# The last conv block's taps as fp32r products on TensorE, and the taps of the last two blocks dealt anew

## The chip, the cores and the metric

The kernel runs on one core of a Trainium2 chip. A core has five engines with a queue each, and every queue is worked through in its own order: TensorE (PE in the profile, with PEld for the loading of its weights), VectorE (DVE), ScalarE (ACT), GpSimd (POOL) and SyncE (SP). They wait for each other on semaphores. The metric is the device time of one execution in microseconds (us), the median of several runs.

## What is computed

A trunk of two layers on 256 tokens of width 2048, all in float32. Layer 0 mixes tokens with a Conformer convolution module, layer 1 with latent attention; each is followed by a squared-ReLU MLP. The change lies in the convolution module of layer 0:

```python
def conv_module(h, w_pw1, b_pw1, w_dw, b_dw, ln_g, ln_b, w_pw2, b_pw2):
    u = h @ w_pw1 + b_pw1
    a, gate = jnp.split(u, 2, axis=-1)
    u = a * jax.nn.sigmoid(gate)
    u = depthwise_causal_conv(u, w_dw, width=31) + b_dw
    u = jax.nn.silu(layer_norm(u, ln_g, ln_b))
    return u @ w_pw2 + b_pw2
```

The depthwise convolution gives, for each of the 2048 channels, the sum of 31 taps: each is that channel's row of u, shifted by 0 to 30 tokens, times a weight of its own. The LayerNorm behind it is over all 2048 channels of a token, so nothing behind it can start before the last channel is done.

## The kernel before

Large products run on TensorE in fp32r. A float32 operand x is split into an upper part hi (ScalarE, a copy into fp32r, `upper_half`) and the rest lo = x - hi (`lower_half`), and a product is three of fp32r parts: hi by hi, lo by hi, hi by lo.

The convolution module goes through 16 blocks of 128 channels. In pass c of the loop (c = 1 to 16) TensorE computes both halves of the pointwise product for block c (`conv_mm`, 96 products of 256 columns; the second half starts with row 8), while the other engines work on the block before:

- `glu(c - 1)`: ScalarE takes the sigmoid of the gate (`sg`) and copies the other half (`vb`), GpSimd multiplies them into `ub`, a row of 30 zeros and 256 tokens. For blocks 0, 14 and 15 VectorE does the last step itself (L844).
- The 31 taps of the block are dealt out. ScalarE starts two sums in PSUM with taps 0 and 1 (`start_sum`, L880) and computes a few side products into SBUF (`tp`, `SIDE`: one per block, 2 for block 13, 4 for block 14), which GpSimd adds up (`side_sum`). VectorE adds the others one by one into the two sums (`add_tap`, L910); the last step of the second sum goes into `half` in SBUF, and GpSimd adds the side products to that (`side_join`). At the end VectorE adds the first sum and `half` into `ca` (L918). `SECOND_END` says how many taps are left for the first sum when the second one ends; these are done in the next pass, alternating with the next block's.
- ScalarE and GpSimd split the weights for the coming products (`conv_half`, 8 rows of two loads to a half: `hi` on ScalarE, `lo` on GpSimd).
- Now and then the finished blocks are transposed (`to_tokens`) for the LayerNorm's mean and variance (`ln_stats`: on ScalarE for blocks up to 13, with `bn_stats` on VectorE for 14 and 15).

Block 15 has no product of a later block beside it. 15 of its taps are therefore done on TensorE: ScalarE prepares 15 diagonal matrices `dg` (the identity, scaled by the tap's weight, L862; 8 in pass 13, 7 in pass 14), and TensorE multiplies each, in plain float32, with `ub` shifted (L873), summing in PSUM. ScalarE starts the sum with tap 15, VectorE adds taps 16 to 23 to it in turn with the rest of block 14, and ScalarE and GpSimd make and add the last 7. VectorE puts the three together (`half` at L1163, `ca` at L1166); then come the transposes and statistics of blocks 14 and 15, the mean and the reciprocal deviation (`rsqrt`), which TensorE spreads over the partitions (`spread`, L1213), normalisation and swish, and the product with `w_pw2` (L1287), whose first weights were split at the end of pass 15.

The instructions of the module stand in the order in which the code is written (`tc.manual_schedule()`): each engine's queue has the order of the calls, whichever engine they are for. An engine whose next instruction waits does nothing else. Since `dve_taps(c - 1)` puts all the steps of a pass on VectorE's queue at once, VectorE and ScalarE can be at different passes at the same time.

## Time and profile before

| | us |
|---|---|
| median of 3 runs (1933.84 to 1935.36) | 1934.36 |
| the profiled execution's own time | 1934.31 |
| its span | 1932.5 |
| pass 13 begins: ScalarE's `sg` for block 12 | 163.10 |
| VectorE's `ub` for block 15 | 198.87 |
| first product with `w_pw2` (L1287) | 210.61 |

Times are from the start of the span. The profiled execution took 1.8 us more than its span, and 0.05 us less than the median. A row of the timeline reads: start, length, engine, line and operation, output and inputs with their shapes, how many of the same stand in a row, and in brackets how long the engine stood idle before and what ended that. Lengths of neighbouring instructions overlap a little: an engine begins the next one before the last one's result is out. A row of the chain of waits reads: start, length, engine and output. A row of the table by stretches has, for each engine, the busy time with the number of instructions, then TensorE's granted clock (1.00 is full speed), the share of the DMA engines and GB/s.

### The profile page before, as it was taken

Reading aid. Unit: us, or ns where it says so; the run is one execution under the profiler, and the core shown is the slowest. Engines: PE = TensorE matmul, PEld = TensorE weight load, DVE = VectorE, ACT = ScalarE, POOL = GpSimd, SP = SyncE. Lnnn points to the kernel's source line nnn. Section 1 sums busy time; section 2 is a strip of 40 time slices with the busy share of each in tenths; the row PEclk is TensorE's granted clock in tenths of the full one; section 3 lists DMA queues with packets and bytes.
Section 4 is the critical chain, followed back from the end, with each engine's and each line's share of the span. In section 5 each row is a group of like instructions: output and inputs, shape, how many; then the busy total and the mean of one; then the engine's idle time right before and its main releaser. Section 6 shows DMA issues by size and latency. Waiting matters only on the chain.

```text
span 1932.5 us, 28477 instructions
## 1 busy us (share of the span) xinstructions
PE 1921.0 (99%) x10725; PEld 1681.5 (87%) x10725; DVE 1592.2 (82%) x2457; ACT 1095.6 (57%) x1636; POOL 249.0 (13%) x208
## 2 busy tenths in 40 slices
PE   9999999999999999999999999999999999999998
PEld 8999888888888888888898998888888888888887
DVE  7999988877999776799976766877789987678998
ACT  5667755554555545555576655555555554455554
POOL 6999200000010100000001420000000010000000
PEclk9999999999999999999999999999999999999999
DMA  7766456665585866655656545465646776665774
GB/s 230 214 183 189 153 189 206 193 194 177 175 251 194 263 195 187 194 174 196 217 176 175 142 134 192 155 216 186 188 162 225 222 248 212 191 196 175 231 219 150
DMA packets 230427, 375.50 MB, mean 194 GB/s; under 512 B 16392, under 2 KB 107792, under 8 KB 230032
## 3 DMA queue, kind: packets, MB, share of 16 engines
q1 hardware_dynamic: 224640, 363.28, 58.7%
q0 software_dynamic: 4320, 7.87, 2.2%
q10 hardware_dynamic: 1328, 2.52, 0.4%
q8 instruction: 84, 1.38, 0.3%
q14 instruction: 55, 0.45, 0.1%
HBM read 363.68 MB, written 2.10 MB: 189 GB/s over the span
## 4 chain that ended last, share of the span: by engine, by line
PE 97%; DVE 2%; DMA 0%; ACT 0%; issue 0%; ACTq 0%; DVEq 0%
PE acc L655 24%; PE acc L205 15%; PE acc L203 15%; PE acc L204 15%; PE acc L656 13%; PE acc L823 8%; PE acc L1287 2%; DVE sum L910 1%; DMA xs<-in_x 0%; PE acc L1535 0%; PE acc L1566 0%; PE acc L1565 0%; PE acc L1536 0%; PE acc L1564 0%; PE acc L1537 0%; PE tr L267 0%
## 5 line engine op out<-in xcount | busy, mean ns | idle before, releaser
L174 DVE TENSOR_TENSOR lo<-raw,hi 128x1024 fp32r<-128x1024 f32 (+2 forms) x509 | 602.2, 1197 | 232.3 <-ACT hi L170 226.6
L170 ACT ACTIVATE hi<-raw 128x1024 fp32r<-128x1024 f32 (+2 forms) x574 | 583.9, 1036 | 361.1 <-PE acc L655 203.7
L655 PE MATMUL acc<-xt,hi 128*128 128x512 f32 x2048 | 710.6, 390 | 0.0
L656 PE MATMUL acc<-xt,lo 128*128 128x256 f32 x2048 | 577.5, 282 | 0.0
L655 PEld LDWEIGHTS acc<-xt,hi 128*128 128x128 f32 x2048 | 384.3, 188 | 80.7
L656 PEld LDWEIGHTS acc<-xt,lo 128*128 128x128 f32 x2048 | 387.1, 189 | 0.2
L497 ACT ACTIVATE hi<-raw 128x1024 fp32r<-128x1024 f32 x248 | 228.7, 948 | 228.3 <-DVE raw L505 134.0
L498 DVE TENSOR_TENSOR lo<-raw,hi 128x1024 fp32r<-128x1024 f32 x248 | 263.9, 1087 | 27.6 <-ACT hi L497 22.5
L203 PE MATMUL acc<-hi,sh 128*128 128x512 f32 x514 | 200.1, 389 | 0.0
L205 PE MATMUL acc<-lo,sh 128*128 128x512 f32 x514 | 200.1, 389 | 0.0
L203 PE MATMUL acc<-hi,gh 128*128 128x512 f32 (+1 forms) x516 | 200.0, 388 | 0.0
L205 PE MATMUL acc<-lo,gh 128*128 128x512 f32 (+1 forms) x516 | 199.9, 387 | 0.0
L204 PE MATMUL acc<-hi,gl 128*128 128x512 f32 (+1 forms) x516 | 199.9, 387 | 0.0
L823 PE MATMUL acc<-xt,hi 128*128 128x256 f32 x1024 | 180.2, 281 | 0.3 <-ACT b L1106 0.2
L204 PE MATMUL acc<-hi,sl 128*128 128x512 f32 x450 | 175.1, 389 | 0.0
L578 POOL DMA_DIRECT2D xs<-v x30 | 26.5, 994 | 1136.4 <-DVE lo L174 703.2
L910 DVE SCALAR_TENSOR_TENSOR sum<-ub,w_dw,sum 128x256 f32<-128x256 f32 x409 | 164.3, 481 | 3.6 <-ACT sum L880 3.0
L174 POOL TENSOR_TENSOR lo<-raw,hi 128x1024 fp32r<-128x1024 f32 x65 | 155.0, 2410 | 17.3 <-ACT hi L170 17.3
L823 PEld LDWEIGHTS acc<-xt,hi 128*128 128x128 f32 x1024 | 154.8, 188 | 1.1 <-ACT xt L1090 0.6
L823 PE MATMUL acc<-xt,lo 128*128 128x256 f32 x512 | 139.2, 279 | 0.0
L205 PEld LDWEIGHTS acc<-lo,sh 128*128 128x128 f32 x514 | 96.5, 188 | 20.4 <-DVE lo L498 0.3
L204 PEld LDWEIGHTS acc<-hi,gl 128*128 128x128 f32 x516 | 96.9, 188 | 19.9
(314 smaller groups left out, 2531.3 us busy)
## 6 DMA issues: line engine op xcount, KB each, us to landing
raw<-in_mlp_w SPq DMA_DIRECT2D x255, 1024.0 KB, 5.5
raw<-in_conv_w_pw SPq DMA_DIRECT2D x62, 512.0 KB, 5.1
raw<-in_conv_w_pw SPq DMA_DIRECT2D x16, 1024.0 KB, 5.1
raw<-in_mla_w_o SPq DMA_DIRECT2D x16, 1024.0 KB, 5.7
raw<-in_mla_w_kv_up SPq DMA_DIRECT2D x32, 256.0 KB, 3.9
xs<-v POOLq DMA_DIRECT2D x30, 256.0 KB, 7.8
raw<-in_mla_w_in SPq DMA_DIRECT2D x8, 576.0 KB, 3.8
raw<-in_mla_w_in SPq DMA_DIRECT2D x4, 1024.0 KB
```

Of the source, the lines that this page charges most:

```text
L170: nc.scalar.activation(hi, raw[:, js, :], AF.Copy)
L174: eng.tensor_tensor(lo, raw, hi.bitcast(F32), op=ALU.subtract)
L203: nc.tensor.matmul(ps, sh, mh, start=start, stop=False)
L204: nc.tensor.matmul(ps, sl, mh, start=False, stop=False)
L205: nc.tensor.matmul(ps, sh, ml, start=False, stop=stop)
L497: nc.scalar.activation(hi, src, AF.Copy)
L498: nc.vector.tensor_tensor(lo, src, hi.bitcast(F32), op=ALU.subtract)
L655: nc.tensor.matmul(ps[b], wh[:, bs], xhl(k), start=k == 0, stop=False)
L656: nc.tensor.matmul(ps[b][:, :S], wl[:, bs], xh(k), start=False, stop=k == KC - 1)
L823: nc.tensor.matmul(pss[c][b][:, :S], w[i][:, bs], (xh, xl)[j](k), start=k == i + j == 0, stop=end and k == k0 + nk - 1 and (i, j) == terms ...
L910: nc.vector.scalar_tensor_tensor(out=out, in0=ubs[c][:, w : w + S], scalar=tap(c, w), in1=base, op0=ALU.mult, op1=ALU.add)
L1287: nc.tensor.matmul(ps2[b][t], x_kt(k, t), w[:, bs], start=k == g == i == 0, stop=k == KC - 1 and i == len(group) - 1,)
```

## The change

- The taps of block 15 on TensorE are 14 instead of 15, and no longer float32 products. The 14 weights are split on VectorE into `tap_parts` (a cast to fp32r and a subtraction, 128x14 each, when the first diagonal is made). `dg` holds two matrices per tap, one for each part, so that ScalarE makes 28. They are made in passes 12, 13 and 14 (5, 5 and 4 taps) instead of 13 and 14 (8 and 7). `ub` is split too: the upper part by ScalarE (286 columns) ahead of its other work for the block, the rest by VectorE. TensorE then does 14 products of upper parts, 14 with the lower weights, and, behind the transposes of block 14, 14 with the lower part of `ub`.
- Block 14 gets 9 side products instead of 4, and 2 taps are left for the last pass instead of 7.
- Block 15's other taps: ScalarE starts the sum with tap 14; VectorE adds taps 15 to 24 (10 instead of 8), six to the PSUM sum and four to a second sum in SBUF that begins as ScalarE's product for tap 25; ScalarE makes the products for taps 26 to 30, GpSimd adds them up and then adds VectorE's second sum.
- Transposes of block 14 move ahead of the last 14 products, and its statistics between VectorE's last steps.
- Three weight splits move. The upper part of the last half of the pointwise weights is made ahead of block 14's sums. The lower part of the first half for `w_pw2` moves on GpSimd from behind block 14's side sums to behind block 15's. One upper part for `w_pw2` moves on ScalarE to behind the loading of the square root's table.

```diff
-SIDE = {KC - 3: 2, KC - 2: 4}
-SECOND_END = {KC - 2: 7}
+SIDE = {KC - 3: 2, KC - 2: 9}
+SECOND_END = {KC - 2: 2}
 SIDE_ALL, SECOND_END_ALL, JOIN_AT = 1, 5, 9
-LAST_PE, LAST_DVE = 15, 8
+LAST_PE, LAST_DVE = 14, 10
...
+        ub_parts = [cv.tile([P, PAD + S], F32R, name=nm("ub_part")) for _ in range(2)]
+        tap_parts = [cv.tile([P, LAST_PE], F32R, name=nm("tap_part")) for _ in range(2)]
...
         def diag(c, w):
-            dg = cv2.tile([P, P], F32, tag="dg", name=nm("dg"), bufs=LAST_PE)
-            nc.scalar.activation(dg, ident, AF.Copy, scale=tap(c, w))
+            if w == 0:
+                all_taps = w_dw.rearrange("p (w c) -> p w c", c=KC)[:, :LAST_PE, c]
+                nc.vector.tensor_copy(tap_parts[0], all_taps)
+                nc.vector.tensor_tensor(tap_parts[1], all_taps, tap_parts[0].bitcast(F32), op=ALU.subtract)
+            dg = cv2.tile([P, 2, P], F32R, tag="dg", name=nm("dg"), bufs=LAST_PE)
+            for i in range(2):
+                nc.scalar.activation(dg[:, i, :], ident, AF.Copy, scale=tap_parts[i][:, w : w + 1].bitcast(F32))
             return dg
...
-        def last_products(w0, w1):
-            for w in range(w0, w1):
+        def last_products(i, j):
+            for w in range(LAST_PE):
                 nc.tensor.matmul(
-                    last_sum[0], dgs[w], ubs[KC - 1][:, w : w + S], start=w == 0, stop=w == LAST_PE - 1
+                    last_sum[0], dgs[w][:, i, :], ub_parts[j][:, w : w + S],
+                    start=w == i == j == 0, stop=j == 1 and w == LAST_PE - 1,
                 )
...
             c = KC - 1
             last_sum.append(sum2_tile()[:, :S])
             keep_warm(ident, N_WARM_GAP)
-            last_products(0, LAST_PE)
+            nc.scalar.activation(ub_parts[0], ubs[c], AF.Copy)
+            last_products(0, 0)
+            last_products(1, 0)
             w0 = LAST_PE + 1 + LAST_DVE
             start_sum(c, LAST_PE)
-            sides[c] = [product(c, w) for w in range(w0, W)]
+            sides[c] = [product(c, w) for w in range(w0 + 1, w0 + 3)]
+            pcs[c].append(product(c, w0))
+            sides[c] += [product(c, w) for w in range(w0 + 3, W)]
...
+        def token_stats(c, t):
+            q, p = 2 * t if c < KC - 1 else 0, KC // 2 - 1 + 2 * (c - KC + 2)
+            out = stats[:, t, p : p + 2, :].rearrange("p a b -> p (a b)")
+            nc.vector.bn_stats(out, cts[c][t][:, q * P : (q + 1) * P])
...
                     side_join(KC - 2)
                     to_tokens(KC - 3)
                     start_last()
-                    left[KC - 1] = list(range(LAST_PE + 1, LAST_PE + 1 + LAST_DVE))
-                    dve_step(KC - 2, 0)
-                    dve_taps(KC - 1)
-                    side_sum(KC - 1)
+                    c, taps = KC - 1, list(range(LAST_PE + 1, LAST_PE + 1 + LAST_DVE))
+                    def step_on(i):
+                        add_tap(pcs[c][i], c, taps.pop(0), pcs[c][i])
+                    for _ in range(2):
+                        dve_step(KC - 2, 0)
+                    nc.vector.tensor_tensor(ub_parts[1], ubs[c], ub_parts[0].bitcast(F32), op=ALU.subtract)
+                    step_on(0)
+                    dve_step(KC - 2, 2)
+                    for i in (1, 0, 1, 0, 1, 0, 1):
+                        step_on(i)
+                    to_tokens(KC - 2)
+                    last_products(0, 1)
+                    side_sum(c)
+                    nc.gpsimd.tensor_tensor(sides[c][0], sides[c][0], pcs[c][1], op=ALU.add)
+                    wjs[NU, 0] = lower_half(*uppers[0], nc.gpsimd)
                     ln_stats(KC - 3)
-                    c = KC - 1
+                    step_on(0)
+                    token_stats(KC - 2, 0)
+                    step_on(0)
+                    token_stats(KC - 2, 1)
...
                 pss[c] = [acc_tile() for _ in range(2)]
...
+                if c == KC - 1:
+                    last_half = upper_half(raws[n + 1], 1)
                 start_sum(c - 1)
                 start_sides(c - 1, SIDE.get(c - 1, SIDE_ALL))
                 if c == 1:
                     conv_half(n + 1, 1)
                 else:
                     side_join(c - 2)
-                    conv_half(n + 1, 1)
+                    if c < KC - 1:
+                        conv_half(n + 1, 1)
+                    else:
+                        wjs[n + 1, 1] = lower_half(*last_half, nc.gpsimd)
                 side_sum(c - 1)
...
                 if c == KC - 1:
-                    uppers = [upper_half(raws[NU + i], h) for i in range(2) for h in range(2)]
-                    wjs[NU, 0] = lower_half(*uppers[0], nc.gpsimd)
+                    uppers = [upper_half(raws[NU + i], h) for i, h in ((0, 0), (0, 1), (1, 0))]
...
                 conv_mm(c, 8)
-                if c > KC - 4:
-                    dgs.extend(diag(KC - 1, w) for w in range(len(dgs), min(len(dgs) + 8, LAST_PE)))
+                if c > KC - 5:
+                    dgs.extend(diag(KC - 1, w) for w in range(len(dgs), min(len(dgs) + 5, LAST_PE)))
                 conv_mm(c, 12, end=True)
             warm(AF.Sqrt)
+            uppers.append(upper_half(raws[NU + 1], 1))
             keep_warm(ident, N_WARM_LN[0])
-            to_tokens(KC - 2)
             to_tokens(KC - 1)
-            ln_stats(KC - 2)
             ln_stats(KC - 1)
             keep_warm(ident, N_WARM_LN[1])
             mv = small.tile([P, T, 2], F32, tag="mv", name=nm("mv"))
```

**ScalarE at the end of pass 12.** Before, the statistics of blocks 8 and 9 (`scratch,stats`) are followed by the next pass: `sg` and `vb` of block 12, a weight split and block 12's first sums.

```order
L981 ACTIVATE scratch,stats<-tr_2213,stats 128x256 [waits Activation_49]
L841 ACTIVATE sg_2435<-acc_2273,vecs 128x256 [waits PE_49]
L849 ACTIVATE vb_2437<-acc_2272,vecs 128x256 [waits PE_49]
L170 ACTIVATE hi_2442<-raw_2264 128x1024 [waits DMAHW6_49,DMAHW5_49]
L880 ACTIVATE sum_2446<-ub_121,vecs,w_dw 128x256 [waits DVE_49,Pool_49]
L880 ACTIVATE sum_278_2447<-ub_121,w_dw 128x256 [waits DVE_49]
```

Now ten scalings stand between. These are the first four and what they come behind; six more like them follow.

```order
L999 ACTIVATE scratch,stats<-tr_2217,stats 128x256 [waits Activation_49]
L870 ACTIVATE dg_2414<-ident,tap_part_131 128x128 [waits DVE_49]
L870 ACTIVATE dg_2414<-ident,tap_part_132 128x128 [waits DVE_49]
L870 ACTIVATE dg_2417<-ident,tap_part_131 128x128
L870 ACTIVATE dg_2417<-ident,tap_part_132 128x128
```

And this is where they end:

```order
L870 ACTIVATE dg_2426<-ident,tap_part_132 128x128
L844 ACTIVATE sg_2456<-acc_2277,vecs 128x256 [waits PE_49]
L852 ACTIVATE vb_2458<-acc_2276,vecs 128x256 [waits PE_49]
L170 ACTIVATE hi_2463<-raw_2268 128x1024 [waits DMAHW6_49,DMAHW5_49]
L889 ACTIVATE sum_2467<-ub_121,vecs,w_dw 128x256 [waits Pool_49]
L889 ACTIVATE sum_287_2468<-ub_121,w_dw 128x256
```

The first `dg` waits for VectorE's cast, the second for its subtraction; `sg`, `vb` and the sums of block 12 now stand behind all ten.

**VectorE at the same place of the program.** `half` is the end of block 11's second sum; the rows behind it are block 11's first sum and, in turn with it, block 12's, which waits for ScalarE. Before:

```order
L910 SCALAR_TENSOR_TENSOR sum_2278<-ub_123,w_dw,sum_2278 128x256 [waits DVE_49]
L910 SCALAR_TENSOR_TENSOR half_2317<-ub_123,w_dw,sum_260_2279 128x256 [waits DVE_49]
L910 SCALAR_TENSOR_TENSOR sum_2278<-ub_123,w_dw,sum_2278 128x256 [waits DVE_49]
L910 SCALAR_TENSOR_TENSOR sum_2446<-ub_121,w_dw,sum_2446 128x256 [waits Activation_49]
```

Now:

```order
L923 SCALAR_TENSOR_TENSOR sum_2282<-ub_123,w_dw,sum_2282 128x256 [waits DVE_49]
L923 SCALAR_TENSOR_TENSOR half_2321<-ub_123,w_dw,sum_264_2283 128x256 [waits DVE_49]
L866 CAST tap_part_131<-w_dw 128x14
L867 TENSOR_TENSOR tap_part_132<-w_dw,tap_part_131 128x14 [waits DVE_49]
L923 SCALAR_TENSOR_TENSOR sum_2282<-ub_123,w_dw,sum_2282 128x256
L923 SCALAR_TENSOR_TENSOR sum_2467<-ub_121,w_dw,sum_2467 128x256 [waits Activation_49]
```

The cast and the subtraction have come in behind block 11's `half`.

**VectorE and GpSimd in the last pass.** Here VectorE has the end of block 14 (`ca`) and the last steps of block 15's sum, up to the `half` and `ca` of block 15. Before:

```order
L910 SCALAR_TENSOR_TENSOR sum_2995<-ub_121,w_dw,sum_2995 128x256 [waits DVE_49]
L918 TENSOR_TENSOR ca<-sum_2807,half_2850 128x256 [waits DVE_49,Pool_49]
L910 SCALAR_TENSOR_TENSOR sum_2995<-ub_121,w_dw,sum_2995 128x256 [waits DVE_49] x2
L1163 TENSOR_TENSOR half_3038<-sum_2995,tp_2998 128x256 [waits DVE_49,Pool_49]
L1166 TENSOR_TENSOR ca<-sum_350_2974,half_3038 128x128 [waits DVE_49,PE_49]
L1166 TENSOR_TENSOR ca<-sum_350_2974,half_3038 128x128
```

Now the pass begins like this on VectorE, from `ub` of block 15 to the second step of its sum:

```order
L847 SCALAR_TENSOR_TENSOR ub_121<-acc_2819,vecs,sg_2997 128x256 [waits PE_49,Activation_49]
L923 SCALAR_TENSOR_TENSOR sum_2828<-ub_123,w_dw,sum_2828 128x256
L923 SCALAR_TENSOR_TENSOR sum_2828<-ub_123,w_dw,sum_2828 128x256 [waits DVE_49]
L1180 TENSOR_TENSOR ub_part_130<-ub_121,ub_part_129 128x286 [waits Activation_49]
L923 SCALAR_TENSOR_TENSOR sum_3038<-ub_121,w_dw,sum_3038 128x256 [waits Activation_49]
L931 TENSOR_TENSOR ca<-sum_2828,half_2883 128x256 [waits DVE_49,Pool_49]
L923 SCALAR_TENSOR_TENSOR tp_3045<-ub_121,w_dw,tp_3045 128x256 [waits Activation_49]
L923 SCALAR_TENSOR_TENSOR sum_3038<-ub_121,w_dw,sum_3038 128x256 [waits DVE_49]
```

Block 14's `ca` has moved ahead of all but one of block 15's steps, and four of these (the first is the step into `tp_3045`, which waits for ScalarE's product) now have both inputs in SBUF. On GpSimd the last pass has, after the change, in place of six additions of side products:

```order
L920 TENSOR_TENSOR half_2883<-half_2883,tp_2832 128x256 [waits DVE_49,Pool_49]
L916 TENSOR_TENSOR tp_3041<-tp_3041,tp_3043 128x256 [waits Activation_49]
L916 TENSOR_TENSOR tp_3047<-tp_3047,tp_3049 128x256 [waits Activation_49]
L916 TENSOR_TENSOR tp_3041<-tp_3041,tp_3047 128x256 [waits Pool_49]
L916 TENSOR_TENSOR tp_3041<-tp_3041,tp_3051 128x256 [waits Activation_49,Pool_49]
L1188 TENSOR_TENSOR tp_3041<-tp_3041,tp_3045 128x256 [waits DVE_49,Pool_49]
L174 TENSOR_TENSOR lo_2886<-raw_2690,hi_2885 128x1024 [waits DMAHW7_49,PE_49]
```

The fifth addition waits for the last of VectorE's four steps, and the weight split for `w_pw2` (`lo_2886`) has moved behind it. Behind L1287 the queues are the same as before.

More of the change, by code (lines that the diff above doesn't have):

```diff
@@ L982, in ln_stats @@
                 else:
-                    q, p = 2 * t if c < KC - 1 else 0, KC // 2 - 1 + 2 * (c - KC + 2)
-                    out = stats[:, t, p : p + 2, :].rearrange("p a b -> p (a b)")
-                    nc.vector.bn_stats(out, cts[c][t][:, q * P : (q + 1) * P])
+                    token_stats(c, t)
         for n in range(3):
```

## The prediction

> **What bounds the kernel now.** I read the page first: TensorE is busy 99% of the span, so a change of this size shows only where TensorE waits or its order changes. Then the chain of waits around the changed passes (start, length, what), to see which engine carries the module's end:
>
> ```profile
> span 1932.5 us, 28477 instructions
> ...
> 170.28 5.62 PE acc L823 x48
> ...
> 176.36 1.05 ACT hi L170
> 177.41 0.48 ACT sum L880
> 177.90 0.02 issue
> 177.92 3.29 DVE sum L910 x9
> ...
> 198.87 0.48 DVE ub L844
> ...
> 205.93 0.44 DVE half L1163
> ...
> 210.61 7.74 PE acc L1287 x32
> ```
>
> Up to pass 13 the chain is TensorE's; from 177.9 to 209 it is VectorE's, and with 210.61 TensorE takes over for good. So what VectorE loses between block 11 and the last `ca` goes into the time nearly one for one. Third, VectorE's own timeline:
>
> ```profile
> 159.72 5.96 DVE L910 SCALAR_TENSOR_TENSOR sum<-ub,w_dw,sum 128x256 f32<-128x256 f32 x15
> 165.59 0.47 DVE L910 SCALAR_TENSOR_TENSOR half<-ub,w_dw,sum 128x256 f32<-128x256 f32 x1
> 165.99 4.07 DVE L910 SCALAR_TENSOR_TENSOR sum<-ub,w_dw,sum 128x256 f32<-128x256 f32 x10
> ...
> 177.35 4.19 DVE L910 SCALAR_TENSOR_TENSOR sum<-ub,w_dw,sum 128x256 f32<-128x256 f32 x10
> ...
> 198.38 0.48 DVE L910 SCALAR_TENSOR_TENSOR half<-ub,w_dw,sum 128x256 f32<-128x256 f32 x1
> 198.87 0.48 DVE L844 SCALAR_TENSOR_TENSOR ub<-acc,vecs,sg 128x256 f32<-128x256 f32 x1
> ...
> 206.46 0.49 DVE L1166 TENSOR_TENSOR ca<-sum,half 128x128 f32<-128x128 f32 x2
> 206.86 0.88 DVE L985 BATCH_NORM_STATS2 stats<-acc 128x6 f32<-128x128 f32 x4
> ```
>
> A step takes (5.96 - 0.48) / 14 = 0.39 us, with no gap to spare. The reader should see that block 11's `half` stands at 165.59: VectorE is that far behind. ScalarE's timeline shows how much further ahead it is:
>
> ```profile
> 160.88 0.19 ACT L981 ACTIVATION_READ_ACCUMULATOR scratch<-tr,stats 128x1 f32 x1
> 163.10 0.48 ACT L841 ACTIVATE sg<-acc,vecs 128x256 f32<-128x256 f32 x1 [2.03 <-PE acc L823]
> 164.50 0.48 ACT L849 ACTIVATE vb<-acc,vecs 128x256 f32<-128x256 f32 x1 [0.92 <-PE acc L823]
> 164.87 1.05 ACT L170 ACTIVATE hi<-raw 128x1024 fp32r<-128x1024 f32 x1
> 165.83 0.57 ACT L880 ACTIVATE sum<-ub,vecs,w_dw 128x256 f32<-128x256 f32 x1
> ...
> 169.99 2.44 ACT L862 ACTIVATE dg<-ident,w_dw 128x128 f32<-128x128 f32 x8
> ```
>
> It ends pass 12 at 161.07 and is idle for 2.03 us until the gate of block 12 is there. Into that idle time the change puts ten `dg`.
>
> **The change, part by part.**
>
> *The first ten diagonals: a stall.* The first waits for the cast, and the cast stands on VectorE behind block 11's `half`. That is VectorE's time, not ScalarE's: 165.59 + 0.39 = 165.98. For the cast's length the nearest rows are copies of 32 and of 120 columns:
>
> ```profile
> 4.51 0.19 DVE L1005 COPY vecs<-acc 128x32 f32<-128x32 f32 x1 [3.60 <-PE acc L312]
> 26.81 0.28 DVE L1142 COPY vecs<-sum 128x120 f32<-128x120 f32 x1 [1.47 <-PE sum L312]
> ```
>
> At least nothing, at most 0.28; I take 0.19, since 14 columns are nearest to 32, and 0.04 for the signal: 166.21. The subtraction behind it takes as long and is done before the second `dg` could begin. Ten `dg` at (2.44 - 0.39) / 7 = 0.29 end at 169.14; then `sg`, 0.36 later `vb` at 169.50, where it was at 164.50: **+5.0**. All that hangs on `vb` moves with it: GpSimd's `ub`, ScalarE's `hi`, and block 12's sum, for which VectorE waits one step behind `half`. VectorE therefore stands idle for some 4.5 us from 166.9 and is 5.0 late from there on. If `dg` with fp32r output took its full 0.39, it would be +6.0; a cast in no time gives +4.8.
>
> *TensorE in pass 13.* It needs the second half's weights, whose `hi` is behind that `vb` and whose `lo` is GpSimd's:
>
> ```profile
> 165.05 0.74 POOL L850 TENSOR_TENSOR ub<-vb,sg 128x256 f32<-128x256 f32 x1 [0.17 <-ACT vb L849]
> 166.05 2.42 POOL L174 TENSOR_TENSOR lo<-raw,hi 128x1024 fp32r<-128x1024 f32 x1 [0.26 <-ACT hi L170]
> 168.41 0.77 POOL L907 TENSOR_TENSOR half<-half,tp 128x256 f32<-128x256 f32 x1
> 169.11 7.14 POOL L174 TENSOR_TENSOR lo<-raw,hi 128x1024 fp32r<-128x1024 f32 x3
> ...
> 169.55 0.40 PE L823 MATMUL acc<-xt,hi 128*128 128x256 f32 x2
> ...
> 170.04 0.37 PE L823 MATMUL acc<-xt,hi 128*128 128x256 f32 x1
> ```
>
> TensorE gets there at 170.04; `hi` would come at 170.9 and `lo` at 168.47 + 5.0 = 173.47, so it idles about 3.2 us, and once more 0.3 for the next half. The later halves, up to 5.0 late, come 0.5 to 1.5 before TensorE, itself 3.5 late, needs them. VectorE's `ub` for block 15 waited for its products until 198.87; they now end 3.5 later, at about 202.3, and VectorE gets there at 203.6 (below): the stall is hidden, with 1.3 to spare. DMA:
>
> ```profile
> raw<-in_conv_w_pw SPq DMA_DIRECT2D x62, 512.0 KB, 5.1
> ```
>
> The three raw buffers come free up to 5 us later; a load of 5.1 still lands 3 us or more before its split.
>
> *What VectorE gets back on the way:* the ten rows at 177.35 take 4.19, nine steps and 0.48 only 4.00: a wait of 0.18 for block 13's sum, which comes early enough in the new order (GpSimd's `ub` at 181.2, the sum at 182.5, VectorE there at 182.75). And `ub` of block 15 stood 0.49 behind `half` instead of 0.39, waiting for TensorE: 0.10. `ub` is then at 198.87 + 5.0 - 0.28 = 203.59. Block 14's five taps that leave VectorE are all in the last pass.
>
> *The last pass,* from `ub`'s start, call it U. Rows:
>
> ```profile
> 199.38 0.57 ACT L880 ACTIVATE sum<-ub,vecs,w_dw 128x256 f32<-128x256 f32 x1 [1.46 <-DVE ub L844]
> 199.89 2.89 ACT L855 ACTIVATE tp<-ub,w_dw 128x256 f32<-128x256 f32 x7
> ...
> 200.86 4.51 POOL L903 TENSOR_TENSOR tp<-tp,tp 128x256 f32<-128x256 f32 x6 [0.46 <-ACT tp L855]
> ...
> 199.40 6.75 PE L873 MATMUL sum<-ub,dg 128*128 128x256 f32 x30
> ```
>
> ScalarE: copy of `ub` at U + 0.5 (286 columns, 0.43), sum at U + 0.95, six products from U + 1.46 at 0.40 each. TensorE: 15 float32 products took 6.75; now 28 from U + 1.05 and 14 more, at (169.55 - 169.20) / 3 = 0.117 each (three to a row pair of the pointwise product; quoted is the second of two such pairs), 4.9 and 0.3 for the transposes: ready at U + 6.3, before VectorE asks. VectorE: two steps of block 14, the subtraction, a step, `ca`, then a wait until U + 2.8 for the third product, then eight steps at 0.39 with two statistics of 0.2: U + 6.7. GpSimd: the fourth to sixth products come until U + 3.9; its last four additions at (4.51 - 0.74) / 5 = 0.75 run from U + 3.6 to U + 6.6, and the `half` of block 15 waits for the last: U + 6.7. Before it was 205.93 - 198.87 = 7.06: **-0.36**. GpSimd's eight additions for block 14 end in time: 9 products are there by 198.5, additions from 198.2, done with `side_join` at 205.05, and `ca` of block 14 asks at 205.7.
>
> *The statistics.* Four in a row of 0.2 were wholly VectorE's; now the second of two waits for the last transpose, (206.80 + 0.53) - 206.66 after the last `ca`: **-0.10**.
>
> ```profile
> 206.80 0.53 PE L969 MATMUL acc<-ident,ca 128*128 128x128 f32 x2 [0.33 <-DVE ca L1166]
> ```
>
> *Moved splits.* GpSimd's `lo` for `w_pw2` ends 2.4 after its last addition, at U + 9.0, 2.2 ahead of L1287 (U + 11.2); the `hi` on ScalarE ends 0.3 before the deviation's square root. Nothing, unless the last pass grows by less on the path than on GpSimd.
>
> *Sum:* +5.0 - 0.28 - 0.36 - 0.10 = **+4.26 us**. Behind L1287 the order is unchanged and TensorE carries the path, so nothing gives it back. Against the profiled execution 1934.31 + 4.26 = 1938.57; from the median, 0.05 higher, 1938.6, which is 0.22% more. What a measurement of this kernel can tell from no change is about 0.2%, 3.9 us: 1938.2.
>
> **The rivals.**
>
> *VectorE and GpSimd block each other (slower still).* Before, each step of VectorE beside GpSimd reads one operand from PSUM (`sum`), so the trace cannot show what two SBUF operands do. Now the subtraction and four steps have two. If such a step and an addition of 0.74 exclude each other, the first step waits 0.35 for the first addition, and the later three alternate with the additions that the `half` waits for, each pushing the other by 0.35 to 0.4: 1.4 in all, 1940.0. It decides from the first overlap on, at U + 2.8. Against it: VectorE's and GpSimd's rows above run beside each other at full speed, but only with one operand each. The Trainium skill, SBUF — State Buffer, section "Who interferes with whom", says just this: an instruction of VectorE with two SBUF inputs contends with one of GpSimd that reads SBUF, through a shared read interface, and whichever comes second blocks. No row here shows it; by that page the sum would be this rival's.
>
> *TensorE's clock falls in the stall (slower still).*
>
> ```profile
> 168.00:172.00 4.00, 4.00 (x37) 4.00 (x36) 4.00 (x12) 4.00 (x10) 4.00 (x4) 1.00 0.51 150
> 208.00:212.00 4.00, 3.51 (x23) 2.75 (x22) 2.93 (x13) 3.69 (x7) 0.00 (x0) 1.00 0.00 0
> ```
>
> The granted clock (behind GpSimd's busy time) is 1.00 in these stretches, and TensorE's longest pause between them is the 0.33 above. A pause of 3.2 is new. At half speed for as long as that, products lose 1.7, of which 1.3 are covered; twice as long, 3.4: 1939.0 to 1940.7. The page TensorE: Matmul & The Clock Gate of the Trainium skill (section "What's actually happening") puts half speed behind a whole idle window of about 3.4 us; a pause of 3.2 with two products in it would just miss that.
>
> *ScalarE does not stall (no slower).* If the cast ran before ScalarE gets there, ten `dg` of 2.9 would fit into the 2.03 and the wait before `vb` of 0.92. That needs the cast by 161.6; then only cast and subtraction (0.25) come on VectorE's path, mostly covered by the 0.28 of waits, and the last pass keeps its -0.46: 1933.9. For it, the cast needs nothing from block 11; against it, the order puts it behind `half_2321`, and VectorE's rows have that at 165.59.
>
> **How the numbers follow.** The forecast 55%, 1938.0 to 1939.6 by the bounds of cast, `dg` and last pass; blocked ports 24%; the clock 8%; no stall 8%; other sizes 5%. The point is the forecast's. From 1937.9, half a us under the least stall, to 1940.6, past the blocked ports: a little under 9 in 10 with the forecast's and both slower rivals' shares. Slower by over 0.2%: four fifths of the forecast, nearly all of the slower rivals, 78%; within 0.2%: the rest of the forecast and no stall, 20%; faster by over 0.2%, which no term gives, 2%.
>
> **What would show it.** In the changed kernel's ScalarE timeline the ten `dg` begin at about 166.2, not 161.1, with 5 us of idle time ahead of them put down to VectorE's cast, and `sg` follows at 169.1; VectorE has a gap of about 4.5 us behind 166.9; TensorE one of about 3 in pass 13. `ub` of block 15 stands near 203.6, L1287 near 214.9. `dg` rows at 161.1 would make the forecast wrong at its root; VectorE's SBUF steps longer than 0.5, or additions longer than 0.8, would show the blocked ports, a granted clock under 1.00 the gate.

## The result: 0.3% slower, and the profile after

The changed kernel takes 1940.2 us (median of 8 runs, 1939.26 to 1940.63) against 1934.47 for the kernel before (8 runs, 1933.84 to 1935.36): a ratio of 1.0029, interval 1.0019 to 1.0038. Its profiled execution took 1939.26 us, with a span of 1937.5, 5.0 more than before.

The chain of waits of the changed kernel, in the changed passes (start, length, what):

```profile
165.43 0.38 DVE half L923
165.93 0.27 ACT dg L870
166.24 2.73 ACT dg L870 x9
...
203.29 0.49 DVE ub L847
...
210.71 0.42 DVE half L1195
...
215.30 2.83 PE acc L1322 x11
```

Up to pass 13 the chain was TensorE's. It now runs through block 11's `half` on VectorE and the ten `dg` on ScalarE behind it. ScalarE's timeline shows the idle time and what ended it:

```profile
160.62 0.19 ACT L999 ACTIVATION_READ_ACCUMULATOR scratch<-tr,stats 128x1 f32 x1
165.93 3.04 ACT L870 ACTIVATE dg<-ident,tap_part 128x128 fp32r<-128x128 f32 x10 [5.12 <-DVE tap_part L866]
168.88 0.45 ACT L844 ACTIVATE sg<-acc,vecs 128x256 f32<-128x256 f32 x1
169.24 0.46 ACT L852 ACTIVATE vb<-acc,vecs 128x256 f32<-128x256 f32 x1
```

VectorE's timeline has the cast, the gap that follows one step later, and the last pass:

```profile
165.34 0.47 DVE L923 SCALAR_TENSOR_TENSOR half<-ub,w_dw,sum 128x256 f32<-128x256 f32 x1
165.73 0.17 DVE L866 CAST tap_part<-w_dw 128x14 fp32r<-128x14 f32 x1
...
171.13 3.62 DVE L923 SCALAR_TENSOR_TENSOR sum<-ub,w_dw,sum 128x256 f32<-128x256 f32 x9 [4.63 <-ACT sum L889]
...
203.29 0.48 DVE L847 SCALAR_TENSOR_TENSOR ub<-acc,vecs,sg 128x256 f32<-128x256 f32 x1
...
204.60 0.56 DVE L1180 TENSOR_TENSOR ub_part<-ub,ub_part 128x286 fp32r<-128x286 f32 x1
...
205.97 0.66 DVE L923 SCALAR_TENSOR_TENSOR tp<-ub,w_dw,tp 128x256 f32<-128x256 f32 x1
...
206.95 0.89 DVE L923 SCALAR_TENSOR_TENSOR tp<-ub,w_dw,tp 128x256 f32<-128x256 f32 x1
...
208.15 0.57 DVE L923 SCALAR_TENSOR_TENSOR tp<-ub,w_dw,tp 128x256 f32<-128x256 f32 x1
...
209.03 0.56 DVE L923 SCALAR_TENSOR_TENSOR tp<-ub,w_dw,tp 128x256 f32<-128x256 f32 x1
...
210.71 0.41 DVE L1195 TENSOR_TENSOR half<-sum,tp 128x256 f32<-128x256 f32 x1
```

This execution has block 11's `half` 0.25 us earlier than the one of before (165.34 against 165.59), ahead of everything that the change moves. So times are compared from that `half` on: to the first product with `w_pw2` it was 210.61 - 165.59 = 45.02, and it is 215.30 - 165.34 = **49.96, 4.94 more**. This breaks up at the start of block 15's `ub` and at its `half`: up to `ub` 37.95 against 33.28 (+4.67), from `ub` to `half` 7.42 against 7.06 (+0.36), from there 4.59 against 4.68 (-0.09).

GpSimd's timeline of the last pass: its join of block 14, its four additions of products, and the one that waits for VectorE.

```profile
204.11 0.73 POOL L920 TENSOR_TENSOR half<-half,tp 128x256 f32<-128x256 f32 x1
205.62 0.73 POOL L916 TENSOR_TENSOR tp<-tp,tp 128x256 f32<-128x256 f32 x1 [0.77 <-ACT tp L858]
206.82 2.50 POOL L916 TENSOR_TENSOR tp<-tp,tp 128x256 f32<-128x256 f32 x3 [0.47 <-ACT tp L858]
209.74 0.72 POOL L1188 TENSOR_TENSOR tp<-tp,tp 128x256 f32<-128x256 f32 x1 [0.43 <-DVE tp L923]
```

TensorE's timeline has two waits in pass 13, and in the last pass some idle time on either side of its products:

```profile
170.69 0.50 PE L826 MATMUL acc<-xt,hi 128*128 128x256 f32 x2 [0.66 <-ACT hi L170]
173.18 0.58 PE L826 MATMUL acc<-xt,lo 128*128 128x256 f32 x1 [1.99 <-POOL lo L174]
...
204.30 3.62 PE L881 MATMUL sum<-ub_part,dg 128*128 128x256 f32 x28 [0.54 <-ACT ub_part L902]
...
211.57 0.53 PE L982 MATMUL acc<-ident,ca 128*128 128x128 f32 x2 [1.65 <-DVE ca L1198]
```

The table by stretches (the granted clock stands behind GpSimd's busy time) shows that the clock fell:

```profile
172.00:173.00 1.00, 0.00 (x0) 0.00 (x0) 1.00 (x4) 1.00 (x2) 1.00 (x1) 0.96 0.00 0
173.00:174.00 1.00, 0.82 (x4) 0.82 (x5) 1.00 (x4) 1.00 (x2) 1.00 (x3) 0.50 0.00 0
174.00:175.00 1.00, 1.00 (x6) 1.00 (x6) 1.00 (x4) 1.00 (x3) 1.00 (x1) 0.50 0.00 0
175.00:176.00 1.00, 1.00 (x7) 1.00 (x6) 1.00 (x4) 1.00 (x5) 1.00 (x1) 0.50 0.00 0
176.00:177.00 1.00, 1.00 (x9) 1.00 (x9) 1.00 (x4) 1.00 (x4) 1.00 (x2) 0.83 0.00 0
```

Three questions follow. Is the stall all of the 4.67? What makes VectorE's steps into `tp` 0.56 to 0.89 long, where those into `sum` take 0.48? And is the fallen clock behind the spread of the 8 runs, which lie in two groups (1939.26 to 1939.60, and 1940.18 to 1940.63)?

### The profile page after: what moved, and what is told of

Its sections match the earlier page's. It is cut to its first block, busy times and chain, and to the rows that moved or that the text cites. A ratio compares the mean times of both kernels' runs of the same rounds, so it can differ in the third digit from the quotient of the medians.

```text
span 1937.5 us, 28519 instructions
## 1 busy us (share of the span) xinstructions
PE 1921.0 (99%) x10737; PEld 1681.7 (87%) x10737; DVE 1591.6 (82%) x2457; ACT 1100.7 (57%) x1654; POOL 251.8 (13%) x212
## 4 chain that ended last, share of the span: by engine, by line
PE 96%; DVE 3%; ACT 1%; DMA 0%; issue 0%; ACTq 0%; DVEq 0%
PE acc L655 24%; PE acc L205 15%; PE acc L204 15%; PE acc L203 15%; PE acc L656 13%; PE acc L826 7%; PE acc L1322 2%; DVE sum L923 2%; DMA xs<-in_x 0%; PE acc L1570 0%; PE acc L1601 0%; PE acc L1599 0%; PE acc L1600 0%; PE acc L1571 0%; PE acc L1572 0%; PE tr L267 0%
## 5 line engine op out<-in xcount | busy, mean ns | idle before, releaser
L203 PEld LDWEIGHTS acc<-hi,gh 128*128 128x128 f32 x516 | 96.9, 188 | 19.9
```

Source lines behind the costliest of these rows:

```text
L203: nc.tensor.matmul(ps, sh, mh, start=start, stop=False)
```

## The experiments

The kernel before took 1934.34 us (30 runs) beside the first four kernels, 1934.11 (19 runs) beside the next four and 1934.50 (12 runs) beside the last.

### The cast early

```diff
+        def split_taps(c):
+            all_taps = w_dw.rearrange("p (w c) -> p w c", c=KC)[:, :LAST_PE, c]
+            nc.vector.tensor_copy(tap_parts[0], all_taps)
+            nc.vector.tensor_tensor(tap_parts[1], all_taps, tap_parts[0].bitcast(F32), op=ALU.subtract)
...
         def diag(c, w):
-            if w == 0:
-                all_taps = w_dw.rearrange("p (w c) -> p w c", c=KC)[:, :LAST_PE, c]
-                nc.vector.tensor_copy(tap_parts[0], all_taps)
-                nc.vector.tensor_tensor(tap_parts[1], all_taps, tap_parts[0].bitcast(F32), op=ALU.subtract)
...
+                if c == 1:
+                    split_taps(KC - 1)
```

> The changed kernel, with the cast and the subtraction of the 14 weights moved from VectorE's place behind block 11's half to the end of pass 1. Theory A (ScalarE's wait for the cast is the loss): the ten dg begin at about 161 and sg of block 12 at about 164; no wait on VectorE is left, TensorE's granted clock stays at 1.00, and what is left against the kernel before is the last pass, 7.42 instead of 7.06 us from ub to half, less 0.1 for the statistics: 1934.7. Theory B (the last pass with its SBUF steps and blocked ports is the loss): the wait was covered, and the time stays over 1938.

Measured: 1935.25 us (11 runs, 1934.46 to 1936.4), ratio 1.0005, interval 0.9996 to 1.0014. ScalarE's timeline of this kernel:

```profile
160.71 3.03 ACT L871 ACTIVATE dg<-ident,tap_part 128x128 fp32r<-128x128 f32 x10
163.64 0.47 ACT L844 ACTIVATE sg<-acc,vecs 128x256 f32<-128x256 f32 x1
164.25 0.47 ACT L852 ACTIVATE vb<-acc,vecs 128x256 f32<-128x256 f32 x1
```

The ten diagonals begin without a wait, and fit into idle time that ScalarE had. From block 11's `half` to the first product with `w_pw2` it is 45.27 us, 4.69 less than in the changed kernel. The granted clock is 1.00 throughout these passes. What is left against before, 0.25, is the last pass, 7.42 from `ub` to `half` as in the changed kernel, less the 0.1 of the statistics. So two instructions of less than 0.2 us each, in the wrong place of a queue, are 4.69 of the 4.94 us. By the medians 0.91 us are left, more than the expected 0.4: in this trace the rest lies behind the first product with `w_pw2`, where the kernel takes 0.9 longer than before (see the table further down).

### The stall alone

The kernel before, with its own 15 taps and float32 products; only the first ten diagonals move to pass 12 and wait for a copy on VectorE.

```diff
+            if w == 0:
+                nc.vector.tensor_copy(last_taps, w_dw.rearrange("p (w c) -> p w c", c=KC)[:, :LAST_PE, c])
...
-            nc.scalar.activation(dg, ident, AF.Copy, scale=tap(c, w))
+            nc.scalar.activation(dg, ident, AF.Copy, scale=last_taps[:, w : w + 1])
...
-                if c > KC - 4:
-                    dgs.extend(diag(KC - 1, w) for w in range(len(dgs), min(len(dgs) + 8, LAST_PE)))
+                if c > KC - 5:
+                    dgs.extend(diag(KC - 1, w) for w in range(len(dgs), min(len(dgs) + 10, LAST_PE)))
```

> The kernel before, in which the first ten of its 15 float32 diagonals are made at the end of pass 12 and scaled by a copy of the weights that VectorE makes just then (the other five in pass 13). Nothing else is changed. Theory A: ScalarE waits for the copy until about 166.2, block 12's sg begins at 169.1, and of the 5.0 us 4.7 arrive: 1939.2, up to 1940.2 where the clock falls in TensorE's wait. Theory B: under 1936.

Measured: 1939.32 us (10 runs, 1938.74 to 1940.48), ratio 1.0025, interval 1.0016 to 1.0035. ScalarE's and then VectorE's timeline:

```profile
165.96 3.03 ACT L866 ACTIVATE dg<-ident,last_taps 128x128 f32<-128x128 f32 x10 [5.11 <-DVE last_taps L864]
```

```profile
165.37 0.47 DVE L914 SCALAR_TENSOR_TENSOR half<-ub,w_dw,sum 128x256 f32<-128x256 f32 x1
165.76 0.17 DVE L864 COPY last_taps<-w_dw 128x15 f32<-128x15 f32 x1
...
203.32 0.48 DVE L844 SCALAR_TENSOR_TENSOR ub<-acc,vecs,sg 128x256 f32<-128x256 f32 x1
...
210.38 0.42 DVE L1167 TENSOR_TENSOR half<-sum,tp 128x256 f32<-128x256 f32 x1
```

`half` to `ub` is 37.95, as in the changed kernel, and the last pass 7.06, as before. The stall by itself makes the 4.67. TensorE has the same two waits here (0.64 and 1.98), and the clock falls to 0.50 as well.

### TensorE kept busy in the stall, and the changed kernel again

28 transposes of the identity, into a part of a tile that is written afresh later, stand ahead of the products that wait in pass 13:

```diff
+                if c == KC - 3:
+                    for _ in range(28):
+                        nc.tensor.transpose(cts[c - 3][0][:, P : 2 * P], ident, ident)
                 conv_mm(c, 8)
```

> The changed kernel, with 28 transposes of the identity on TensorE (into columns that nothing reads before they are written again) ahead of the second half of pass 13, where it otherwise waits 2.7 us. Theory C (the half clock behind the wait costs the runs that lie near 1940.4 about 1 us, and the ones near 1939.3 nothing): granted clock 1.00 throughout pass 13, median 1939.3 and no run over 1939.8. If the two groups have another cause: median 1940.2, runs from 1939.3 to 1940.6 as before.

Measured: 1939.18 us (9 runs: eight from 1938.88 to 1939.65, one at 1940.68), ratio 1.0026, interval 1.0016 to 1.0035. By the expectation no run should have been above 1939.8. The granted clock is 1.00 from 168 to 184. The changed kernel had been timed apart from this one, so both were run once more on one chip.

> The changed kernel as it is, once more, on the same chip as the next one. Its first runs lay in two groups, 1939.3 to 1939.6 and 1940.2 to 1940.6. If the granted clock that falls in the pause of pass 13 is what makes the upper group (in these runs it falls deeper or longer, and the products for block 15's ub end later than VectorE needs them), the runs lie in the same two groups again, and the next kernel, in which TensorE does not pause, has none above 1939.8; in the profile the products for ub(15) end within 0.3 us of where VectorE asks for it. If the groups are of the chip or of the hour, both kernels show the same spread. If there is nothing but the stall and the slower last pass, 1939.1 to 1939.5 for both.

> The changed kernel with 28 transposes of the identity ahead of the second half's products in pass 13, which keep TensorE busy while it waits, once more beside the changed kernel itself. By the clock: 1939.0 to 1939.4, no run above 1939.8, median 0.5 to 1.0 below the changed kernel's. Without the clock: the same median within 0.2, and as many runs above 1939.8.

Measured: the changed kernel 1939.88 us (6 runs: 1939.62, 1939.72, 1939.82, 1939.93, 1940.51, 1941.84), ratio 1.003, interval 1.0018 to 1.0041; with TensorE kept busy 1939.25 (8 runs, 1939.06 to 1939.80), ratio 1.0026, interval 1.0016 to 1.0036. The medians differ by 0.6 as the clock's theory asked, but the traces that were kept, one for each job, put the difference elsewhere. TensorE's timeline with the transposes, in the second of the two jobs:

```profile
205.05 3.62 PE L881 MATMUL sum<-ub_part,dg 128*128 128x256 f32 x28 [1.66 <-ACT ub_part L902]
```

TensorE is idle for 1.66 here before the first of the last products, against 0.54 in the first trace of the changed kernel. So the low clock costs TensorE some 1.1 us; but this was spare time. Of VectorE's path it takes less than 0.1: in the second trace of the changed kernel `ub` stands 0.47 behind `half` instead of 0.39 or 0.40, and from block 11's `half` to the first product with `w_pw2` it is 50.01 there, against 49.95 in both traces with TensorE kept busy.

What is longer in that trace, a run of 1940.51 us, lies 700 us and more further on: one place is in the MLP of layer 0, the other in the MLP of layer 1. TensorE waits there for VectorE's lower part of a weight (`lo`). TensorE's timeline of the changed kernel, second trace:

```profile
940.57 0.50 PE L205 MATMUL acc<-lo,sh 128*128 128x512 f32 x1 [0.42 <-DVE lo L498]
...
1898.24 0.50 PE L205 MATMUL acc<-lo,sh 128*128 128x512 f32 x1 [0.17 <-DVE lo L498]
```

and that of the kernel with the early cast, in which no clock fell and TensorE did not wait in pass 13:

```profile
1892.96 0.50 PE L205 MATMUL acc<-lo,sh 128*128 128x512 f32 x1 [0.35 <-DVE lo L498]
```

The table holds the two parts of each trace: from block 11's `half` to the first product with `w_pw2`, and from there to the end of the span. "Wait" says whether TensorE's timeline lists one of these waits; shorter ones, such as 0.11 at 1897 us in the changed kernel's first trace, it does not list.

| kernel | `half` to `w_pw2` | from there | wait |
|---|---|---|---|
| before | 45.02 | 1721.9 | no |
| changed | 49.96 | 1722.2 | no |
| changed, again | 50.01 | 1722.9 | yes |
| TensorE busy, both times | 49.95 | 1721.7, 1722.0 | no |
| the stall alone | 49.68 | 1721.9 | no |
| early cast | 45.27 | 1722.8 | yes |
| early cast, 15 taps | 44.91 | 1721.7 | no |
| early cast, 16 taps | 44.74 | 1721.9 | no |
| no side additions | 49.10 | 1723.0 | yes |
| second sum in PSUM | 45.56 | 1721.9 | no |

So the second part takes 1722.8 to 1723.0 us with a listed wait and 1721.7 to 1722.2 without, whatever the first part does. The listed waits are not all of this difference, but it arises at the same two places: beside the first trace with TensorE kept busy, the changed kernel's second trace is 0.2 us later from the module to 936 us, 0.9 from there to 1896, and 1.4 behind that. This makes groups like those of the changed kernel's runs. (The time ahead of block 11's `half`, 165.34 to 166.09 us in these traces, adds to the spread too.) The clock is neither needed for these waits nor enough for them: the early cast has one at a clock of 1.00, and the stall alone has none with a fallen clock. Why some kernels meet them more often is open: 7 of the changed kernel's 14 runs lie above 1940, 1 of 17 with TensorE kept busy, and 1 of 10 of the stall alone, whose clock falls as well. That the other runs above 1940 had these waits is likely, but was not seen, since they have no trace.

### Without GpSimd's additions

```diff
-            sides[c] = [product(c, w) for w in range(w0 + 1, w0 + 3)]
+            sides[c] = [product(c, w) for w in range(w0 + 1, w0 + 2)]
             pcs[c].append(product(c, w0))
-            sides[c] += [product(c, w) for w in range(w0 + 3, W)]
```

> The changed kernel without the taps 27 to 30 of block 15: ScalarE does not make these four products and GpSimd does not add them, so that in the last pass GpSimd has only the join of block 14 and, behind VectorE's four steps into SBUF, one addition. The stall of pass 12 is left as it is. If VectorE's steps with two SBUF operands took 0.56 to 0.89 us, and stood 0.49 to 0.81 apart, because GpSimd was adding beside them, they take 0.48 now and stand 0.39 apart like those into PSUM, and block 15's half comes 6.4 to 6.7 us behind the start of its ub instead of 7.42; time 0.8 under the changed kernel, 1938.4 to 1939.4. If such a step is by itself that much dearer than one into PSUM, the four still take 0.56 to 0.89 and the half stays at 7.1 us or more. The subtraction (two SBUF operands as well) stands beside GpSimd's join of block 14 in both cases and should stay at 0.55 to 0.65 if the former holds.

Measured: one run of 1939.77 us; it has the waits in the MLPs, so it says nothing about 0.8 us. VectorE's timeline decides:

```profile
203.93 0.48 DVE L847 SCALAR_TENSOR_TENSOR ub<-acc,vecs,sg 128x256 f32<-128x256 f32 x1
...
206.51 0.47 DVE L922 SCALAR_TENSOR_TENSOR tp<-ub,w_dw,tp 128x256 f32<-128x256 f32 x1
206.90 0.47 DVE L922 SCALAR_TENSOR_TENSOR sum<-ub,w_dw,sum 128x256 f32<-128x256 f32 x1
207.29 0.47 DVE L922 SCALAR_TENSOR_TENSOR tp<-ub,w_dw,tp 128x256 f32<-128x256 f32 x1
...
210.45 0.40 DVE L1194 TENSOR_TENSOR half<-sum,tp 128x256 f32<-128x256 f32 x1
```

All steps take 0.47 and stand 0.39 apart, and the last pass is 6.52 long. With two SBUF operands a step costs no more than with one; what costs is GpSimd beside it. The last pass is 7.42 - 6.52 = 0.90 us shorter than in the changed kernel, and 0.80 of this lies between the first step into `tp` and `half` (3.94 us instead of 4.74). The rest is for the most part ScalarE's product for that first step, which comes earlier here, since ScalarE's four products are left out with GpSimd's additions. That the steps wait for GpSimd, and not for ScalarE, shows in the changed kernel's trace: when its four steps into `tp` began, the addition that ran on GpSimd had 0.38, 0.61, 0.28 and 0.28 us left, and the steps are 0.19, 0.42, 0.10 and 0.09 longer than 0.47, each time what was left, less 0.19. The subtraction, still beside GpSimd's join, takes 0.62, as expected.

### Fewer SBUF steps: 15 and 16 taps on TensorE

Early cast, and 15 taps on TensorE with 9 on VectorE, three of them into SBUF; then 16 and 8, two of them into SBUF. The diagonals of passes 12 to 14 are for 4, 7 and 4 taps (5 with 16 taps).

```diff
-LAST_PE, LAST_DVE = 14, 10
+LAST_PE, LAST_DVE = 15, 9
...
-                    for i in (1, 0, 1, 0, 1, 0, 1):
+                    for i in (1, 0, 1, 0, 1, 0):
```

> As the first, and one tap more on TensorE (15), one step less on VectorE (9, three of them with both inputs in SBUF instead of four); the diagonals are made 4, 7 and 4 taps to a pass. If an SBUF step beside GpSimd costs 0.49 and TensorE has room (it had finished 0.9 before the last half), the last pass falls to about 6.9 us from ub to half and the time to 1934.2. If TensorE's products become the end of the pass: 1934.7 or more.

> The cast early, as in the kernel with 15 taps on TensorE, but with 16 there (diagonals 4, 7 and 5 per pass), 8 on VectorE and two of these into SBUF instead of three; the buffers for side products one fewer. If VectorE sets the end of the last pass, it is one step of about 0.5 us shorter: 6.55 from the start of block 15's ub to its half instead of 7.05, and TensorE, which has 48 instead of 45 products, ends 0.35 later, at about 7.0 behind ub, just ahead of ca at 7.07; first product with w_pw2 0.5 earlier than in that kernel, time 1933.8. If TensorE takes over as the bound, ca waits for its products and the gain is 0.1 to 0.2: 1934.1 to 1934.2. If the missing buffer delays a product, 1934.3 or more.

Measured: 1934.32 us (11 runs, 1933.77 to 1935.30), ratio 1.0, interval 0.9991 to 1.0009; and 1934.43 (10 runs, 1933.60 to 1936.43), ratio 1.0003, interval 0.9994 to 1.0012. The last pass is 7.05 with 15 taps, where about 6.9 was expected. With 16 it is 6.86 instead of 6.55: neither VectorE nor TensorE sets its end, but GpSimd, for which `half` waits. VectorE's timeline shows this, and the subtraction that gives `ub`'s lower part, which stands beside GpSimd's join of block 14:

```profile
200.20 0.91 DVE L1181 TENSOR_TENSOR ub_part<-ub,ub_part 128x286 fp32r<-128x286 f32 x1
...
205.75 0.42 DVE L1196 TENSOR_TENSOR half<-sum,tp 128x256 f32<-128x256 f32 x1 [0.54 <-POOL tp L1189]
```

GpSimd's row of that join, in this kernel:

```profile
200.06 0.73 POOL L921 TENSOR_TENSOR half<-half,tp 128x256 f32<-128x256 f32 x1
```

With TensorE kept busy, the join is over before the subtraction begins; GpSimd's and VectorE's rows, second job:

```profile
204.56 0.72 POOL L920 TENSOR_TENSOR half<-half,tp 128x256 f32<-128x256 f32 x1
```

```profile
205.34 0.45 DVE L1180 TENSOR_TENSOR ub_part<-ub,ub_part 128x286 fp32r<-128x286 f32 x1
```

The same subtraction takes 0.45 alone, 0.56 when 0.24 of the join are left at its start (the changed kernel), and 0.91 when 0.59 are left (16 taps): each time what was left, less 0.13. The second one waits until the first has all but ended.

### VectorE's second sum in PSUM

If two SBUF operands are what collides, a second sum in PSUM avoids it. 16 taps on TensorE, 9 on VectorE, the second sum in the other half of the first one's bank:

```diff
+            lbank = sum_tile()
+            second = lbank[:, S : 2 * S]
+            pcs[c] = [lbank[:, :S]]
...
-            pcs[c].append(product(c, w0))
+            nc.scalar.activation(second, ubs[c][:, w0 : w0 + S], AF.Copy, scale=tap(c, w0))
+            pcs[c].append(second)
```

> The early cast, 16 taps on TensorE, 9 on VectorE, and VectorE's second sum of block 15 in the other half of the first one's PSUM bank instead of in SBUF: its three steps read one operand from PSUM, the last of them writes to SBUF; GpSimd has three additions of products and the one of that sum. If VectorE's steps were long only through GpSimd's additions beside two SBUF operands, these three take 0.48 and stand 0.39 apart, and block 15's half comes 6.3 to 6.4 us behind the start of its ub (7.05 with 15 taps and the sum in SBUF, 7.06 before, 7.42 in the changed kernel). Then TensorE's 48 products set the end: ca at about 7.15 behind ub instead of 7.57, and 44.4 to 44.6 us from the start of block 11's half to the first product with w_pw2 (45.02 before). Time 0.4 to 0.6 under before, 1933.6 to 1933.9, too little to be told from it in the medians. If two sums in one PSUM bank cost VectorE something, the steps stay at 0.55 or more and half at 6.8 or more.

Measured: 1935.25 us (10 runs, 1934.57 to 1936.25), ratio 1.0004, interval 0.9995 to 1.0014. The expectation missed: the last pass is 206.88 - 199.18 = 7.70 long. VectorE's timeline:

```profile
199.18 0.48 DVE L847 SCALAR_TENSOR_TENSOR ub<-acc,vecs,sg 128x256 f32<-128x256 f32 x1
...
201.83 0.49 DVE L931 SCALAR_TENSOR_TENSOR sum<-ub,w_dw,sum 128x256 f32<-128x256 f32 x1 [0.40 <-ACT sum L915]
...
202.56 2.05 DVE L931 SCALAR_TENSOR_TENSOR sum<-ub,w_dw,sum 128x256 f32<-128x256 f32 x4
...
206.88 0.41 DVE L1207 TENSOR_TENSOR half<-sum,tp 128x256 f32<-128x256 f32 x1
```

The steps are no longer (0.48 and 0.49), so the collision is gone. But they stand (2.05 - 0.48) / 3 = 0.52 apart instead of 0.39, and the first waits 0.40 for ScalarE's start of the *other* sum. Steps that alternate between two halves of one tile follow each other like steps into one sum (two in a row took 1.01 in the changed kernel). Whether the program's waits, which count the bank as one tile, or the bank itself causes it was not tried. No version here beats the kernel before by an amount that its runs can tell.

## Why the prediction was right, and where it was off

The forecast was 1938.6, slower; it came out at 1940.2, inside the range, but above 1939.6, the end of the forecast's own part of it. The stall is what was forecast. That the number stayed inside the range is in part luck: of the 1.6 us above the forecast, 0.7 is the last pass, and most of the rest lies, as far as the traces show it, behind the module, in waits that neither the forecast nor a rival had. The median is near the 1940.0 of the rival with the blocked ports for the same reason, since the ports cost half of what that rival said.

- *The stall, +5.0.* Right in every part. The cast took 0.17 (0.19 predicted). Counted from block 11's `half`, `dg` was to begin 0.62 behind it and began 0.59 behind; `vb` 3.91 and 3.90. It came from the place of block 11's `half` in VectorE's timeline, since the diff shows only two small instructions. The rival without a stall is refuted by ScalarE's 5.12 us of idle time.
- *The waits that VectorE gets back, -0.28.* The stretch to block 15's `ub` grew by 4.67; 5.0 - 0.28 = 4.72. The ten rows that took 4.19 take 4.01, and `ub` stands 0.39 behind `half`, as worked out.
- *The pause in pass 13.* Predicted 3.2 us, hidden with 1.3 to spare. The waits came to 0.66 and 1.99, and the clock did fall, a rival given 8%. It took nearly all of the spare time and then cost under 0.1, not the 0.4 at least that was worked out for it (0.3 by its own terms, since half speed for 3.2 us loses 1.6 and not 1.7): its mechanism was right, its price was not. By the rows above it was at half speed for (1 - 0.96) / 0.5 = 0.08, then 3, then (1 - 0.83) / 0.5 = 0.34: 3.4 us. The Trainium skill, TensorE: Matmul & The Clock Gate, section "What's actually happening", gives the window as about 3.4 us and free-running: the length of the slow stretch agrees, but my reading that two products in the pause keep the clock up is wrong by these rows.
- *The last pass, -0.36.* This is the term that failed: +0.36, because VectorE's five instructions with two SBUF operands wait for GpSimd. The forecast had 6.7 from `ub` to `half`, the measured pass has 7.42; without GpSimd's additions it has 6.52, and 0.80 of the difference is the steps themselves. This is the blocked ports' rival (24%), with the right mechanism and half its price: 0.72 over the forecast against 1.4. It had VectorE and GpSimd push each other in turn; in the rows GpSimd's additions hardly lengthen and VectorE waits for the rest of the one that runs. The Trainium skill, SBUF — State Buffer, section "Who interferes with whom", calls the shared port pair an exclusive lock that the second comer waits for; the subtraction's three lengths agree, but for the last 0.13 us.
- *The statistics, -0.10.* From `half` to the first product: -0.09.
- *Behind L1287, nothing.* Right for the order of the work, and the trace of the changed kernel has 0.3 there. But its second trace has 1.0 there, from waits in the MLPs of both layers, and half of its runs lie as high as such a run: the module gives 4.94, the medians 5.73. The forecast took the profiled execution's tail for that of every run.

The sum with the measured terms is 4.67 + 0.36 - 0.09 = 4.94, or 1939.3 by the profiled execution of before; the profiled execution of the changed kernel took 1939.26.

## What to carry to other kernels

Where an engine runs ahead of another, read from the trace how far, before giving it an instruction that needs something from the one behind: an operation of 0.17 us cost 4.7, because its queue was five microseconds late, and moved to the first pass it cost nothing that the trace can show. Counting instructions would have called that part of the change free. An instruction of VectorE with two operands in SBUF wants a moment in which GpSimd is not adding: keep one operand in PSUM, with a tile to each sum, or count the rest of GpSimd's instruction into each step. And a difference of half a microsecond in the medians can come from a wait 700 us further on; compare stretches of the traces, not their ends.

## What was not expected of the hardware

- The granted clock fell after waits of 0.66 and 1.99 us with two products between them, in every trace that had this pause, and was 0.50 for 3.4 us each time.
- A VectorE step into one sum follows its predecessor into the same sum after 0.52 us, and one into another sum after 0.39. Steps into two halves of one tile in a PSUM bank, in turn, stood 0.52 apart like steps into the same sum; whether the waits for the tile or the bank make this was not tried.
- A subtraction of 128x286 took 0.45, 0.56 or 0.91 us, by how much of GpSimd's addition of 0.73 was left when it began; steps of 128x256 with two SBUF operands took 0.47 to 0.89 in the same way.
